# Attention of one decoder layer: dense causal scores per query block, or near key blocks plus key classes modulo 4

## The chip, the cores and the metric

The kernel runs on one core of one Trainium2 chip. The metric is the device time of one execution in microseconds; of the kernel before there are three runs, with a median of 1261.48 us (1261.13 to 1264.27). A core has one matrix engine (TensorE; PE in the profile, its weight loads as PEld), VectorE (DVE), ScalarE (ACT), GpSimd (POOL) and SyncE (SP), which issues the DMAs. Each engine works through its own queue in the order in which the program was written; semaphores hold an instruction until what it needs is there.

## The reference

One decoder layer on 1024 tokens of width 1024: RMS norm, one projection into two mixers (8 attention heads of width 64; 4 heads of a gated recurrence of width 128), an output projection, a residual, and a squared-ReLU MLP of width 4096. What the change touches is the attention. Query t sees key t - d with d >= 0 if one of three windows holds it, and the three branches are combined by their softmax denominators, which is one softmax over all keys with a bias that counts the windows:

```python
DILATED_PATTERNS = ((128, 1), (512, 4), (2048, 16))
d = np.arange(P)[:, None] + 896 - np.arange(T)[None, :]
ok = d >= 0
c = ((d <= 128) & ok).astype(np.float64) + ((d <= 512) & (d % 4 == 0) & ok) + ((d % 16 == 0) & ok)
tab[h] = np.where(c > 0, np.log(np.maximum(c, 1.0)) - slope * d, -1.0e30)
```

So for d over 128 only keys of the query's own class modulo 4 count; all others get the bias -1e30.

## The kernel before

The program is written out in full, and the order in which the Python code calls the engines is the order of every queue: a manual schedule. Numbers that need more than the matrix engine's short format are split into a high part and a low part; a product of two split numbers takes three matmuls (`three_pass`, lines 86 to 89), one of a split number and a short one takes two.

The stages are: the norm and the first projections; the four recurrent heads (`hgrn_core`), with projections of the next head filled in between; the attention, 8 heads in 4 pairs; the output projection, row by row of 128 tokens; the MLP.

**The attention loop before** (lines 1016 to 1049) makes 64 steps, one per head and block of 128 queries. In a step with block b:

- `score` multiplies the block's queries with all (b + 1) x 128 keys up to its own, in pieces of at most 512, each with the high and the low part of the keys (lines 703, 704; tile `ps`). VectorE adds the bias and takes the row maximum in one instruction (line 706).
- `expo` (line 717) is one ScalarE exponential over the whole row of keys, with its sum.
- `turn` (line 730, tile `pt`) transposes the weights block by block; ScalarE copies the high part out (`pth`, line 733), VectorE the low part (`ptl`, line 734).
- `weigh` (line 747, tile `pov`) multiplies the values with two query blocks at a time, 256 columns, once for the high and once for the low part.
- `finish` (lines 758 to 763) transposes the result back, adds the two halves and divides by the sum.

Between these steps `fill(ns)` takes work from a queue of generators until their stated costs use up a number of nanoseconds. The work is the projection of the next pair (`attn_proj`: 48 groups of three 512-column matmuls, tiles `pm_aq`, `pm_av`, `pm_ak`) and at the end the first half of the output projection for the first four rows (`early_out`, 32 groups, tile `pwe`). The allowance of a step falls with the block number (line 1045). `hooks` are calls tied to a step number: they load and split the weights of the output projection (`w_get`) and prepare its rows.

Biases (`bt`, 512 KB per head, line 683) and weights (`raw`, line 104) come by DMA on SyncE's queue. The two halves of q, kh and kl are also copied between the partitions of a pair's two heads by DMA (lines 589, 590, 619, 620).

Of the kernel before, what the change touches and what calls it, by code (L numbers as in the profile page):

```python
# [35 lines left out]
def hymba_layer(ctx, tc, x, w_in, w_out, w_ff1, w_ff2, g_pre, lb_logits, g_mix, g_post,  # L36
# [114 lines left out]
    for i in range(4 * HH, 4 * HH + 3 * (AH // 2)):  # L151
        stream.append((w_in[i], None))
    WO0 = len(stream)
    WO_TAG = (None, None, ("S", "S"), ("S", "BT"), ("S", "S"), ("S", "T"), ("T", "T"), ("T", "T"))
# [262 lines left out]
    def hgrn_core(h, scale, after=None):  # L417
# [143 lines left out]
        fill(1500 * scale)  # L561
# [8 lines left out]
    first_done = [False] * (AH // 2)  # L570
    A0 = 4 * HH

    put_off = []

    def keys_read(pr, pm, hf):
# [3 lines left out]
        return full  # L579

    def keys_off(pr, stacks, full, hf):

        sl = slice(hf * 512, hf * 512 + 512)
# [8 lines left out]
    def keys_late():  # L592
        while put_off:
            pr, stacks, src, hf, read = put_off.pop()
            keys_off(pr, stacks, src if read else keys_read(pr, src, hf), hf)

    def keys_early_read():
        pr, stacks, src, hf, _ = put_off.pop()
        put_off.append((pr, stacks, keys_read(pr, src, hf), hf, True))

    def attn_proj(pr):
# [5 lines left out]
        for hf in range(2):  # L607
            sl = slice(hf * 512, hf * 512 + 512)
            for n, cost in enumerate(proj_t(w, f"aq{pr}", hf, box)):
                if hf == 0 and n == 4:  # L610
                    w_get(A0 + 3 * pr)
                yield cost
# [8 lines left out]
            yield 650.0  # L621
        w = w_get(A0 + 3 * pr + 1, 0)
        vs = slab("V8", f"v{pr}", F32R, (P, NT, 2, 2, 64))
        late = None

        def v_turn(full, hf):
            pt = bank("mm", f"pvt{pr}{hf}")
            for j in range(4):
                TE.transpose(pt[:, j * P:(j + 1) * P], full[:, j * P:(j + 1) * P], ident)
            ptv = pt.rearrange("p (j h d) -> p j h d", j=4, h=2)  # L630
            dst = vs[:, hf * 4:hf * 4 + 4]
            S.activation(dst[:, :, :, 0, :], ptv, AF.Copy)
            V.tensor_tensor(out=dst[:, :, :, 1, :], in0=ptv, in1=f32(dst[:, :, :, 0, :]), op=ALU.subtract)
        for hf in range(2):
            sl = slice(hf * 512, hf * 512 + 512)
            n = 0
            for cost in proj_t(w, f"av{pr}", hf, box):
                n += 1
                if n == 4 and late is not None:
                    v_turn(*late)  # L640
                    cost += 450.0
                if n == 5 and hf == 0:
                    w_get(A0 + 3 * pr + 1)
# [4 lines left out]
            yield 650.0  # L648
        while pr > 0 and not first_done[pr - 1]:
            yield None  # L650
        w = w_get(A0 + 3 * pr + 2, 0)
        for i in range(2):
            stacks[i]["kh"] = slab("S", f"kh{pr}_{i}", F32R)
            stacks[i]["kl"] = slab("S", f"kl{pr}_{i}", F32R)
        for hf in range(2):
            sl = slice(hf * 512, hf * 512 + 512)
            n = 0
            for cost in proj_t(w, f"ak{pr}", hf, box):
                n += 1
                if n == 3 and hf == 0:  # L660
                    v_turn(*late)
                    cost += 450.0
                if n == 6 and hf == 0:
                    w_get(A0 + 3 * pr + 2)
                yield cost
            if hf == 0 and pr == AH // 2 - 1:
                early_rows()
            if hf == 0:
                keys_off(pr, stacks, keys_read(pr, box[0], hf), hf)
            else:  # L670
                put_off.append((pr, stacks, box[0], hf, False))
            pairs[pr] = (stacks, vs)
            yield 650.0

    anats = [None] * (AH // 2)
    bts = {}
    stats = {}
    pts = {}

    def load_bias(hd):  # L680
        if hd < AH and hd not in bts:
            bts[hd] = slab("BT", f"bt{hd}") if hd < AH - 1 else early["table"][:, 0]
            nc.sync.dma_start(out=bts[hd], in_=bias_tab[hd])

    def score(hd, b):
        stacks, _ = pairs[hd // 2]
        if b == 0:
            load_bias(hd)
            if hd + 1 < AH - 1:
                load_bias(hd + 1)  # L690
            stats[hd] = {n: tp.tile([P, NT, 2] if n == "mx" else [P, NT], F32, tag=n, name=f"{n}{hd}", bufs=2)
                         for n in ("mx", "nm", "dn", "rd")}
        q, kh, kl = (stacks[hd % 2][n] for n in ("q", "kh", "kl"))
        nk = (b + 1) * P
        mx, nm = stats[hd]["mx"], stats[hd]["nm"]
        pe = slab("P", f"p{hd}_{b}")
        pieces = []
        qs = q[:, b * P:(b + 1) * P]
        for pc in range(1 if nk <= 512 else 2):
            k0 = pc * 512  # L700
            n = min(512, nk - k0)
            pS = bank("s", f"ps{hd}_{b}_{pc}")
            TE.matmul(pS[:, :n], qs, kh[:, k0:k0 + n], start=True, stop=False)
            TE.matmul(pS[:, :n], qs, kl[:, k0:k0 + n], start=False, stop=True)  # L704
            o = 896 - b * P + k0
            V.tensor_tensor_reduce(out=pe[:, k0:k0 + n], in0=pS[:, :n], in1=bts[hd][:, o:o + n], scale=1.0,  # L706
                                   scalar=-3.0e38, op0=ALU.add, op1=ALU.max, accum_out=mx[:, b, pc:pc + 1])
            pieces.append((k0, n))
        if len(pieces) == 1:
            V.tensor_scalar(nm[:, b:b + 1], mx[:, b, 0:1], -1.0, None, op0=ALU.mult)  # L710
        else:
            V.tensor_scalar(nm[:, b:b + 1], mx[:, b, 0:1], mx[:, b, 1:2], -1.0, op0=ALU.max, op1=ALU.mult)
        return pe, nk

    def expo(hd, b, pe, nk):
        nm, dn = stats[hd]["nm"], stats[hd]["dn"]
        S.activation(pe[:, :nk], pe[:, :nk], AF.Exp, bias=nm[:, b:b + 1], accum_out=dn[:, b:b + 1])  # L717
        return pe

    def turn(hd, b, pe):  # L720
        g, u = divmod(b, 2)
        if u == 0:
            ns = (2 * g + 5) // 4
            pts[hd, g] = [[slab("T", f"pt{q}{hd}_{g}_{s}", F32R, (P, 4, 256)) for q in "hl"] for s in range(ns)]
        for s in range((b + 4) // 4):
            nj = min(4, b + 1 - 4 * s)
            pt = bank("t", f"pt{hd}_{b}_{s}")
            for j in range(nj):
                jj = s * 4 + j
                TE.transpose(pt[:, j * P:(j + 1) * P], pe[:, jj * P:(jj + 1) * P], ident)  # L730
            src = pt[:, :nj * P].rearrange("p (j c) -> p j c", j=nj)
            hi, lo = (q[:, :nj, u * P:(u + 1) * P] for q in pts[hd, g][s])
            S.activation(hi, src, AF.Copy)  # L733
            V.tensor_tensor(out=lo, in0=src, in1=f32(hi), op=ALU.subtract)  # L734
        dn, rd = stats[hd]["dn"], stats[hd]["rd"]
        V.reciprocal(rd[:, b:b + 1], dn[:, b:b + 1])

    def weigh(hd, g):
        _, vs = pairs[hd // 2]
        pt = pts.pop((hd, g))  # L740
        po = bank("pv", f"pov{hd}_{g}")
        nj = 2 * g + 2
        for j in range(nj):
            c0 = P if j == nj - 1 else 0
            vst = vs[:, j, hd % 2].rearrange("p a d -> p (a d)")
            for q in range(2):
                TE.matmul(po[:, c0:256], vst, pt[j // 4][q][:, j % 4, c0:],  # L747
                          start=j == 0 and q == 0, stop=j == nj - 1 and q == 1)
        ot = sp.tile([P, 256], F32, tag="ot", name=f"ot{hd}_{g}", bufs=1)
        S.activation(ot, po[:, :256], AF.Copy)  # L750
        return po, ot

    def finish(hd, g, po, ot):
        pr = hd // 2
        if anats[pr] is None:
            anats[pr] = slab("T", f"anat{pr}", F32, (P, NT, 2, 64))
        for u in range(2):
            TE.transpose(po[:, 256 + u * P:256 + (u + 1) * P], ot[:, u * P:(u + 1) * P], ident)
        pair = po[:, 256:].rearrange("p (u a d) -> p u a d", u=2, a=2)
        b = slice(2 * g, 2 * g + 2)  # L760
        dst = anats[pr][:, b, hd % 2]
        V.tensor_reduce(dst, pair.rearrange("p u a d -> p u d a"), axis=AX.X, op=ALU.add)  # L762
        G.tensor_tensor(out=dst, in0=dst, in1=stats[hd]["rd"][:, b].unsqueeze(2).to_broadcast([P, 2, 64]),  # L763
                        op=ALU.mult)
        if hd % 2 and g == NT // 2 - 1 and pr < AH // 2 - 1:
# [1130 lines left out]
```

## Time and profile before

| | |
|---|---|
| three runs | 1261.13, 1261.48, 1264.27 us |
| the profiled execution, span | 1258.5 us |
| PE busy | 1235.4 us (98%) |
| DVE, ACT, POOL busy | 884.6 (70%), 531.9 (42%), 300.6 us (24%) |
| DMA, share of 16 engines | 36.0% on the queue that SyncE issues |
| the attention loop in the profile | 307 us to 557 us |

The profiled execution's span is 3.0 us under the median of the runs. "Busy" of PE counts each matmul with the time that its result needs to come out, and these overlap: matmuls that follow each other can each last longer than the distance between their starts. The distance of two starts is what a matmul costs in a sequence. Time in which PE waits less than that overlap shows as no idle time at all.

### The profile page before, as it was taken

The page shows a single profiled execution, that of the slowest core. Times are in us where ns is not written, and L with a number is a line of the kernel's source. Part 1 is how long each engine was busy: PE and PEld are TensorE (multiplying, and loading weights), DVE is VectorE, ACT ScalarE, POOL GpSimd, SP SyncE. Part 2 cuts the span into 40 slices and gives each one's busy share as a digit, 9 for nine tenths or more (in the row PEclk, how much of TensorE's full clock was granted, in tenths as well). Part 3 has the DMA queues.
Part 4 walks back from the last instruction along what each step waited for, and adds up shares of the span by engine and source line. Part 5 has one row for each costly group of instructions (what it writes and reads, how often), then busy time and mean ns, then how long its engine had stood idle before and what let it go on. Part 6 is the DMA issues. An engine that isn't in the chain of part 4 may idle for free. (4 is left out here: it accounts for less than half of the span.)

```text
span 1258.5 us, 17252 instructions
## 1 busy us (share of the span) xinstructions
PE 1235.4 (98%) x6512; PEld 1056.1 (84%) x6512; DVE 884.6 (70%) x1535; ACT 531.9 (42%) x970; POOL 300.6 (24%) x303
## 2 busy tenths in 40 slices
PE   8999999999999999999999999999999999999997
PEld 8898989888888887878878788888878888888886
DVE  5686868675666667668759756666685777698966
ACT  7523232222555556666565322222237434444412
POOL 0000000012222223146250487656621000000012
PEclk9999999999999999999999999999999999999999
DMA  5201111122322224245242545434468454434423
GB/s 210 68 18 51 34 52 34 35 84 64 89 71 81 69 83 132 81 133 184 101 150 81 207 164 184 155 135 172 149 249 324 167 198 134 162 92 132 162 89 118
DMA packets 58578, 153.98 MB, mean 122 GB/s; under 512 B 4992, under 2 KB 12928, under 8 KB 58240
## 3 DMA queue, kind: packets, MB, share of 16 engines
q1 hardware_dynamic: 58496, 152.89, 36.0%
q8 instruction: 51, 0.84, 0.3%
q14 instruction: 31, 0.25, 0.1%
HBM read 106.73 MB, written 39.85 MB: 116 GB/s over the span
## 5 line engine op out<-in xcount | busy, mean ns | idle before, releaser
L87 PE MATMUL f<-bh,ah 128*128 128x512 f32 x392 | 152.5, 389 | 0.0
L88 PE MATMUL f<-bl,ah 128*128 128x512 f32 x392 | 152.5, 389 | 0.0
L89 PE MATMUL f<-bh,al 128*128 128x512 f32 x392 | 152.5, 389 | 0.0
L84 DVE TENSOR_TENSOR al<-ar,ah 128x1024 fp32r<-128x1024 f32 x49 | 60.7, 1238 | 48.1 <-ACT ah L83 19.4
L89 PEld LDWEIGHTS f<-bh,al 128*128 128x128 f32 x392 | 73.6, 188 | 15.4
L87 PEld LDWEIGHTS f<-bh,ah 128*128 128x128 f32 x392 | 73.6, 188 | 15.3
L88 PEld LDWEIGHTS f<-bl,ah 128*128 128x128 f32 x392 | 73.6, 188 | 15.1
L83 ACT ACTIVATE ah<-ar 128x1024 fp32r<-128x1024 f32 x49 | 52.1, 1063 | 50.2 <-PE f L89 25.3
L1814 POOL TENSOR_SCALAR fp<-fss 128x1 f32<-128x1 f32 x8 | 3.7, 462 | 269.4 <-ACT fd L1810 269.4
L734 DVE TENSOR_TENSOR ptl<-pt,pth 128x512 fp32r<-128x512 f32 (+2 forms) x96 | 50.4, 553 | 23.4 <-ACT pth L733 23.3
L733 ACT ACTIVATE pth<-pt 128x512 fp32r<-128x512 f32 (+2 forms) x96 | 43.3, 487 | 40.0 <-PE pt L730 38.5
L706 DVE CUSTOM_DVE_ANT_0 p<-ps,bt 128x512 f32<-128x512 f32 (+2 forms) x84 | 44.4, 554 | 18.3 <-PE ps L704 18.1
L1313 POOL TENSOR_TENSOR e<-x,e 128x512 f32<-128x512 f32 x14 | 20.6, 1475 | 136.0 <-DVE x L1264 136.0
L79 POOL TENSOR_SCALAR ms<-hss 128x8 f32<-128x8 f32 x4 | 0.8, 198 | 209.2 <-DVE hss L554 209.2
L717 ACT ACTIVATE p<-p,nm 128x128 f32<-128x128 f32 (+3 forms) x64 | 49.4, 772 | 2.5 <-DVE nm L710 2.1
L83 ACT ACTIVATE bh<-br 128x1024 fp32r<-128x1024 f32 x28 | 29.8, 1064 | 43.1 <-PE f L89 37.7
L763 POOL TENSOR_TENSOR anat<-anat,rd 128x128 f32<-128x128 f32 x32 | 14.7, 461 | 131.8 <-DVE anat L762 130.9
L730 PE MATMUL pt<-ident,p 128*128 128x128 f32 x288 | 42.7, 275 | 2.7 <-DVE ptl L734 1.6
L747 PE MATMUL pov<-pth,v 128*128 128x256 f32 (+1 forms) x160 | 40.3, 287 | 1.3 <-ACT pth L733 1.3
L1667 DVE TENSOR_TENSOR acc<-f,acc 128x512 f32<-128x512 f32 x52 | 33.8, 686 | 8.2 <-PE f L89 8.2
L730 PEld LDWEIGHTS pt<-ident,p 128*128 128x128 f32 x288 | 33.3, 141 | 7.2 <-DVE ptl L734 3.5
L83 ACT ACTIVATE bh<-tt 128x1024 fp32r<-128x1024 f32 x21 | 22.3, 1061 | 38.2 <-PE f L89 22.9
(1622 smaller groups left out, 3902.3 us busy)
## 6 DMA issues: line engine op xcount, KB each, us to landing
ar<-actd SPq DMA_DIRECT2D x49, 512.0 KB, 3.7
raw<-in_w_in_dram SPq DMA_DIRECT2D x28, 512.0 KB, 3.6
w1r<-in_w_ff_dram SPq DMA_DIRECT2D x14, 1024.0 KB, 6.2
br<-in_w_ff_dram SPq DMA_DIRECT2D x14, 1024.0 KB, 7.9
actd<-e SPq DMA_DIRECT2D x17, 768.0 KB, 4.1
actd<-e SPq DMA_DIRECT2D x11, 1024.0 KB, 4.0
xr<-in_x_dram SPq DMA_DIRECT2D x8, 512.0 KB, 8.6
raw<-in_w_out_dram SPq DMA_DIRECT2D x8, 512.0 KB, 3.6
```

The costliest lines, as they stand in the source:

```text
L83: S.activation(hi, src, AF.Copy)
L84: eng.tensor_tensor(out=lo, in0=src, in1=f32(hi), op=ALU.subtract)
L87: TE.matmul(dst, lhs[0], rhs[0], start=start, stop=False)
L88: TE.matmul(dst, lhs[0], rhs[1], start=False, stop=False)
L89: TE.matmul(dst, lhs[1], rhs[0], start=False, stop=stop)
L706: V.tensor_tensor_reduce(out=pe[:, k0:k0 + n], in0=pS[:, :n], in1=bts[hd][:, o:o + n], scale=1.0, scalar=-3.0e38, op0=ALU.add, op1=ALU.max ...
L717: S.activation(pe[:, :nk], pe[:, :nk], AF.Exp, bias=nm[:, b:b + 1], accum_out=dn[:, b:b + 1])
L730: TE.transpose(pt[:, j * P:(j + 1) * P], pe[:, jj * P:(jj + 1) * P], ident)
L733: S.activation(hi, src, AF.Copy)
L734: V.tensor_tensor(out=lo, in0=src, in1=f32(hi), op=ALU.subtract)
L747: TE.matmul(po[:, c0:256], vst, pt[j // 4][q][:, j % 4, c0:], start=j == 0 and q == 0, stop=j == nj - 1 and q == 1)
L1667: V.tensor_tensor(out=acc_at(p, i), in0=pm, in1=acc_at(p, i), op=ALU.add)
```

## The change

The queries of the first half (blocks 0 to 3) keep their dense scores. A query block of the second half is scored in two parts. The **near** part takes whole key blocks: keys 384 to 639 for block 4, 512 to 767 for block 5, 512 to 895 for block 6, 512 to 1023 for block 7. The **class** part takes the 512 queries of the second half and the 512 keys of the first half, both sorted by their number modulo 4, and multiplies only like with like: four products of 128 queries with 128 keys.

A query now has two row maxima in two layouts: by block (query 128 b + p on partition p) and by class (query 4 m + c on partition m). `exchange` writes both to DRAM and reads each back in the other layout, `shift` takes the larger of the two, and so both parts use one maximum. `sums` sends the sum of the class part the same way, and `recip` adds the two before the division.

Weighted values are now formed by key block: one transposed key block of all the query blocks that see it (up to 512 columns) against that block's values. In the second half the columns are kept in class order by a permuted unit matrix, `spare["turn"]`, and the values of the first half are also turned in class order (`vc`, four more transposes per pair). Keys are projected before values.

The loop is written new. There is one unit of work per head and half: `near_slot` for the first half's unit, `far_slot` for the second's, four steps each, so 64 steps again. Between pieces stands `yield 1`, at which one group of the queue is issued (`pump`), three per step; from step 46 on the rate is 0.67 of that. The one `fill` behind the last recurrent head is gone, and six groups are issued before the loop instead. The bias table is cut to what is read and comes in five DMAs per head. Hook numbers, and which buffers the output projection's first weights take, are moved.

```diff
@@ attn_proj: keys before values, values of the first half also by class
+        vc = slab("T", f"vc{pr}", F32R, (P, 4, 2, 2, 64))
...
+                TE.transpose(pt[:, j * P:(j + 1) * P], by_class(full)[:, j] if kind else full[:, j * P:(j + 1) * P], ident)
@@ tables, near key blocks, classes
+    FAR = ((384, 256), (512, 256), (512, 384), (512, 512))
+    def load_table(hd):
+        t = tabs[hd] = slab("BT", f"tab{hd}") if hd < AH - 1 else early["table"][:, 0]
...
+        nc.sync.dma_start(out=t[:, :512], in_=bias_tab[hd][:, 512:])
+        G.memset(t[:32, 896:], -1.0e30)
+        for b in range(4):
+            nc.sync.dma_start(out=t[32 * b:32 * b + 32, 512:1024 if b else 896], in_=src[:, 384 - P * b:896 - P * b if b else 768])
+    def score(hd, *blocks):
...
+        for b in blocks:
+            k0, n = keys_of(b)
+            two(pS[:, o:o + n], q[:, b * P:(b + 1) * P], kh[:, k0:k0 + n], kl[:, k0:k0 + n])
...
+    def score_classes(hd):
...
+        for c in range(4):
+            two(pS[:, c], by_class(q[:, 512:])[:, c], by_class(kh[:, :512])[:, c], by_class(kl[:, :512])[:, c])
...
+            row_max(probs["c"][:, c], pS[:, c], tab, unit(2 * hd + 1)["mx"][:, 4 + c:5 + c])
+    def exchange(u):
+        r = unit(u)
+        xd = dp.tile([2, 512], F32, name=f"xd{u}")
+        nc.sync.dma_start(out=xd[0].rearrange("(b p) -> p b", b=4), in_=r["mx"][:, :4])
+        nc.sync.dma_start(out=xd[1].rearrange("(m c) -> m c", c=4), in_=r["mx"][:, 4:])
+        nc.sync.dma_start(out=r["nm"][:, 4:], in_=xd[0].rearrange("(m c) -> m c", c=4))
+        nc.sync.dma_start(out=r["nm"][:, :4], in_=xd[1].rearrange("(b p) -> p b", b=4))
+    def shift(u):
...
+        if u % 2:
+            V.tensor_tensor(out=r["mx"], in0=r["mx"], in1=r["nm"], op=ALU.max)
+        V.tensor_scalar(r["nm"][:, w], r["mx"][:, w], -1.0, None, op0=ALU.mult)
@@ weighted values by key block: (key block, first query block, place in the turned tile, query blocks)
+    SUMS = (([(0, 0, 0, 4)], [(1, 1, 0, 3)], [(2, 2, 0, 2), (3, 3, 2, 1)]),
+            ([(4, 0, 0, 4)], [(5, 1, 0, 3), (3, 0, 3, 1)], [(6, 2, 0, 2), (7, 3, 2, 1)], None))
@@ the loop
-        fill(3240.0 - 340.0 * b if s < n_steps - 20 else 1000.0 if s < n_steps - 16 else 1175.0 if s != n_steps - 3 else 1.0,
-             b == 7 and s < n_steps - 20)
+    EARLY_GROUPS, LATE_FROM = 6, 46
+    LATE_RATE = (0.67,) * (n_steps - LATE_FROM)
+    def near_slot(hd):
...
+        score(hd, 7)
+        score_classes(hd)
+        exchange(u + 1)
...
+            load_table(nxt)
+        yield 1
+        turn(u, 1)
+        yield 1
+        weigh(u, 0)
+        yield 1
+        yield 0
+        turn(u, 2)
+        yield 1
+        weigh(u, 1)
+        yield 1
+        yield 1
+        yield 0
+        weigh(u, 2)
+        gather(u)
+        recip(u)
+        shift(u + 1)
+        expo(u + 1, 0, 1, 2, 3)
+        yield 1
+        yield 1
+        yield 1
+        yield 0
+    def far_slot(hd):
...
+            scores_d(nxt, 0)
+        yield 1
+        finish(u - 1)
+        yield 1
+        turn(u, 0)
...
```

How the rows of PE change: of the kernel before, one step of the loop, with the scores of block 5 against 768 keys in two pieces, four turned pieces of block 3 and a run of fillers (`pm_ak` is the projection, `pt` the turned weights):

```order
L703 MATMUL ps_5_0_4888<-kh_1_4072,q_1_3618 128x512
L704 MATMUL ps_5_0_4888<-kl_1_4073,q_1_3618 128x512
L703 MATMUL ps_5_1_4892<-kh_1_4072,q_1_3618 128x256
L704 MATMUL ps_5_1_4892<-kl_1_4073,q_1_3618 128x256
L730 MATMUL pt_3_0_4897<-ident,p_3_4788 128x128 x4
L758 MATMUL pov_0_4843<-ident,ot_0_4848 128x128 x2
L87 MATMUL pm_ak_4882<-hTh_92,wh_4595 128x512
L88 MATMUL pm_ak_4882<-hTl_93,wh_4595 128x512
L89 MATMUL pm_ak_4882<-hTh_92,wl_4596 128x512
```

And of the changed kernel the second step of a near slot: block 7 against 512 keys, the class scores, then groups of fillers between the pieces (`pm_av` is the projection, `pov` the weighted values):

```order
L704 MATMUL ps_7_3369<-kh_1_2667,q_1_2549 128x512
L705 MATMUL ps_7_3369<-kl_1_2668,q_1_2549 128x512
L704 MATMUL psc_3373<-kh_1_2667,q_1_2549 128x128
L705 MATMUL psc_3373<-kl_1_2668,q_1_2549 128x128
...
L87 MATMUL pm_av_3326<-hTh_90,wh_3187 128x512
L88 MATMUL pm_av_3326<-hTl_91,wh_3187 128x512
L89 MATMUL pm_av_3326<-hTh_90,wl_3188 128x512
L797 MATMUL pt_1_3408<-ident,prob_2544 128x128
L797 MATMUL pt_1_3408<-ident,prob_2948 128x128 x2
...
L818 MATMUL pov_3417<-pt_0_3349,v_2787 128x512 x2
```

Fewer and in part wider matmuls stand there, and eight narrow ones (the `psc` pair comes four times) that the kernel before does not have.

On SyncE's queue the kernel before has one bias load per head between the copies of kl and the next weights:

```order
L590 DMA kl_1_3364<-kl_1_3364 64x512
L683 DMA bt_3605<-in_bias_tab_dram 128x1024
L589 DMA kh_0_3361<-kh_0_3361 64x512
L590 DMA kh_1_3363<-kh_1_3363 64x512
L589 DMA kl_0_3362<-kl_0_3362 64x512
```

The changed kernel has there, once per head, the exchange of the maxima (`umx` to DRAM `xd`, `xd` to `unm`), five loads of the table, and before the next head the sums (`udn`, `nd`, `udd`):

```order
L744 DMA xd_3386<-umx_3335 128x4x1
L745 DMA xd_3386<-umx_3335 128x4
L746 DMA unm_3336<-xd_3386 128x4
L747 DMA unm_3336<-xd_3386 128x4x1
L677 DMA tab_3391<-in_bias_tab_dram 128x512
L680 DMA tab_3391<-in_bias_tab_dram 32x384
L680 DMA tab_3391<-in_bias_tab_dram 32x512 x3
L104 DMA raw_3405<-in_w_in_dram 128x1024
L766 DMA nd_3538<-udn_3337 128x4
L767 DMA udd_3338<-nd_3538 128x4x1
```

The reads from `xd` stand behind the writes, so they hold the queue until these have landed; the table and the next weights stand behind the reads.

On VectorE the larger maximum is taken in queue order, between other heads' and other pieces' work:

```order
L801 TENSOR_TENSOR pt_2_3423<-pt_2_3424,pt_2_3423 128x384
L663 TENSOR_TENSOR vf_3433<-pm_av_3326,rrow 128x512
L650 TENSOR_TENSOR v_3324<-pvt_3444,v_3324 128x8x64
L775 RECIPROCAL urd_3181<-udn_3179 128x4
L753 TENSOR_TENSOR umx_3335<-umx_3335,unm_3336 128x8
L754 TENSOR_SCALAR unm_3336<-umx_3335 128x8
L650 TENSOR_TENSOR vc_3325<-pvt_3469,vc_3325 128x8x64
L708 ISA prob_2948,umx_3484<-ps_0_3479,tab_3391 128x128
```

Line 753 waits for the exchange, and the rest of VectorE's queue stands behind it; in the kernel before, the maximum of a block is used on the spot and no DMA lies between.

More of the change, by code (lines that the diff above doesn't have):

```diff
@@ L647, in attn_proj @@
             late = (full, hf)
[L648 to L665, printed above, removed]
@@ L715, in expo @@
[L715 to L736, printed above, removed]
@@ L759, in finish @@
[L759 to L765, printed above, removed]
+        po = r["po"]
+        for j in range(4):
+            TE.transpose(po[:, j * P:(j + 1) * P], spare["ot"][:, j * P:(j + 1) * P], ident)
```

402 lines of the change are left out of this document (259 added, 143 removed).

## The prediction

> **What bounds the kernel now.** I read the page first, then the sums of the attention stage, then who makes PE wait there.
>
> ```profile
> span 1258.5 us, 17252 instructions
> ...
> PE 1235.4 (98%) x6512; PEld 1056.1 (84%) x6512; DVE 884.6 (70%) x1535; ACT 531.9 (42%) x970; POOL 300.6 (24%) x303
> ```
>
> ```profile
> core 0: us, PE busy (x) PEld busy (x) DVE busy (x) ACT busy (x) POOL busy (x), PEclk, DMA share, GB/s
> 307.00:557.00 250.00, 242.72 (x1449) 211.57 (x1448) 164.99 (x502) 148.66 (x330) 62.84 (x78) 0.99 0.28 82
> ```
>
> ```profile
> PE pmt L848 <- POOL erows L808: 2.9, 1, 2.9
> PE pt L730 <- DVE ptl L734: 1.6, 4, 1.0
> PE pov L747 <- ACT pth L733: 1.3, 1, 1.3
> PE pt L730 <- DVE mt L84: 1.0, 1, 1.0
> PE pov L747 <- DVE ptl L734: 0.3, 1, 0.3
> ```
>
> In the 250 us of the attention PE is busy for 242.7, VectorE for 165.0, ScalarE for 148.7, and all of PE's waits are 7.1 us (2.9 + 1.6 + 1.3 + 1.0 + 0.3). So matmuls taken out here shorten the stage, as long as the other engines and the DMAs still deliver in time.
>
> **What a matmul costs** is the distance to the next start, read in one stretch of the timeline (start, duration, instruction):
>
> ```profile
> 400.12 1.03 PE L730 MATMUL pt<-ident,p 128*128 128x128 f32 x8
> ...
> 401.68 0.40 PE L89 MATMUL pm_av<-hTh,wl 128*128 128x512 f32 x1
> 401.91 0.34 PE L703 MATMUL ps<-kh,q 128*128 128x384 f32 x1
> 402.09 0.34 PE L704 MATMUL ps<-kl,q 128*128 128x384 f32 x1
> ...
> 404.19 0.28 PE L747 MATMUL pov<-pth,v 128*128 128x256 f32 x1
> 404.31 0.28 PE L747 MATMUL pov<-ptl,v 128*128 128x256 f32 x1
> 404.43 0.22 PE L747 MATMUL pov<-pth,v 128*128 128x128 f32 x1
> 404.49 0.28 PE L747 MATMUL pov<-ptl,v 128*128 128x128 f32 x1
> 404.60 0.45 PE L87 MATMUL pm_av<-hTh,wh 128*128 128x512 f32 x1
> 404.88 0.39 PE L88 MATMUL pm_av<-hTl,wh 128*128 128x512 f32 x1
> ```
>
> 512 columns take 0.23 us (401.68 to 401.91), 384 take 0.18, 256 take 0.12. A transpose takes (1.03 - 0.28) / 7 = 0.108, its own duration being about that of a narrow matmul. Of the narrow pair the first takes 0.06, the second 0.11, and the matmul behind it is 0.05 late (0.28 where 0.23 is usual): 0.11 each. So narrow matmuls are dear: 128 columns cost almost what 256 do.
>
> **The matmuls, part by part.** The counts follow from the code. Per head, before, the scores are 12 of 512 columns and 4 each of 384, 256 and 128; after, they are 4 of 512, 4 of 384, 6 of 256 and 10 of 128 (eight of them classes): -8 x 0.23 + 2 x 0.12 + 6 x 0.11 = -0.94 us. The weighted values are 32 of 256 and 8 of 128 before (4.72 us); after, 4 of 512, 4 of 384, 4 of 256 and 14 of 128 (0.92 + 0.72 + 0.48 + 1.54 = 3.66 us): -1.06. Turned weights are 36 pieces before and 25 after: -11 x 0.108 = -1.19. Over 8 heads -7.5, -8.5 and -9.5. The values turned by class add 16 transposes, +1.7. Turning the results back stays at 8 transposes per head. The fillers stay what they are: 144 projection groups and 32 output groups move between steps, and the `fill` behind the last recurrent head only hands its groups to the loop. Sum: **-23.8 us**.
>
> **The other engines** keep their cover. Their rows:
>
> ```profile
> L734 DVE TENSOR_TENSOR ptl<-pt,pth 128x512 fp32r<-128x512 f32 x48 | 32.4, 689 | 16.3 <-ACT pth L733 16.3
> ...
> L706 DVE CUSTOM_DVE_ANT_0 p<-ps,bt 128x512 f32<-128x512 f32 x42 | 28.4, 688 | 14.2 <-PE ps L704 14.2
> L733 ACT ACTIVATE pth<-pt 128x512 fp32r<-128x512 f32 x48 | 27.7, 595 | 23.1 <-PE pt L730 21.5 <-POOL anat L763 1.2
> ...
> L717 ACT ACTIVATION_READ_ACCUMULATOR p<-p,nm 128x1 f32 x64 | 12.1, 189 | 0.0
> ...
> L706 DVE DVE_READ_ACCUMULATOR2_ANT mx<- 128x1 f32 x96 | 8.0, 83 | 0.0
> ...
> L717 ACT ACTIVATE p<-p,nm 128x512 f32<-128x512 f32 x8 | 5.7, 714 | 0.4 <-DVE nm L710 0.4
> ...
> L710 DVE TENSOR_SCALAR nm<-mx 128x1 f32<-128x1 f32 x32 | 4.9, 154 | 1.1
> L717 ACT ACTIVATE p<-p,nm 128x384 f32<-128x384 f32 x8 | 4.9, 611 | 0.1
> ...
> L717 ACT ACTIVATE p<-p,nm 128x256 f32<-128x256 f32 x8 | 4.1, 510 | 0.1
> ...
> L706 DVE CUSTOM_DVE_ANT_0 p<-ps,bt 128x128 f32<-128x128 f32 x14 | 4.0, 286 | 0.2
> ```
>
> VectorE loses about as many score columns as PE and keeps 12 row maxima per head; ScalarE's exponentials go from 8 to 12 per head, of narrower rows, and four more reads of the sum (4 x 0.19 us) are paid by fewer copied pieces. Neither comes near the share that PE has, so their work costs nothing; what may cost is when it is done.
>
> **The added wait: the exchange of the maxima.** Four small DMAs through DRAM, two hops in a row. Nothing that small is in this trace; the nearest landings:
>
> ```profile
> kl<-kl SPq DMA_DIRECT2D x16, 128.0 KB, 2.4
> ...
> ident<-in_ident_dram SPq DMA_DIRECT2D x1, 64.0 KB, 1.9
> gpre<-in_g_pre_dram SPq DMA_DIRECT2D x1, 4.0 KB, 3.4
> ```
>
> A hop lies between 1.9 us (`ident`) and 3.4 (`gpre`, few bytes in 128 pieces, behind other loads). I take 2.4, the row of this stage that is also a partition-wise shuffle; the exchange's pieces of 4 bytes speak for more.
>
> Now the chain of one head, counted from the moment PE starts block 7 in the near slot. Score 7 costs 0.46 us on PE, and its row maximum can begin 0.16 later (a 512-column result takes 0.39 for a distance of 0.23) and ends at 0.62 + 0.69 + 0.08 = 1.39; four class maxima of 0.29 + 0.08 end at 2.9. Two hops of 2.4: 7.7. Two small operations of 0.15 on VectorE: 8.0. Four exponentials (0.51 + 0.51 + 0.61 + 0.71 and 4 x 0.19): 11.1. Then PE may turn the first pieces of the second half.
>
> PE itself gets there after the rest of that step (0.46 + 8 x 0.11 + 3 groups of 0.69 + 3 transposes + 2 x 0.23 = 4.2 us), the next (0.32 + 0.36 + 2.07 = 2.75), the next (0.24 + 0.22 + 2.07 = 2.53) and the head of the far slot (0.46 + 0.43 + 1.38 = 2.27): 11.7 us. So the wait ends 0.6 us ahead, for six heads. Heads 6 and 7 have only 0.67 of the groups: 11 x 0.33 x 0.69 = 2.5 us less, and PE is there at 9.2, 1.9 us too early. What is queued behind the wait: on VectorE the low parts and the next head's row maxima, on SyncE the table, weights and sums; PE waits for all of them only a step later.
>
> Price: 2 x 1.9 = 3.8 us in the last two heads, and half a microsecond each in the other six for copies and weights ahead of the exchange in the queue: 7 us. Against it, 3.2 of the 7.1 us of waits go (the ones on `pth` and `ptl`): every turned piece now has two groups or more ahead of its use. The waits on `erows` and `mt` (3.9) belong to the output rows, which are prepared as before. Net **+4**. At 1.9 us a hop the six heads are covered and the last two lose 0.9 each: -1. At 3.4 a hop the chain ends at 13.1: 1.4 x 6 + 3.9 x 2 = 16.2, net +13.
>
> **Strided operands.** The class scores read every fourth column, as weights and as moving data, 64 matmuls, and so do 16 transposes. The nearest row is the last recurrent head's first level, which moves every second column:
>
> ```profile
> L502 PE MATMUL pl<-qt,kt x112: 217/275/275, 259.4 to 293.2; 128*128 128x64 f32 x112
> ```
>
> Minimum, median and maximum show no level that is slower, so I take zero; if a strided load took twice its time, 80 x 0.11 = 9 us.
>
> [...]
>
> **Sum.** 1258.5 - 23.8 + 4 = 1238.7 us for the profiled execution. The median of the three runs (1261.48) lies 3.0 above the profiled span, so 1241.7.
>
> **Rivals.**
>
> *The exchange is slow* (slower than before). From a hop of h the six heads lose 2h - 5.4 each and the last two 2h - 2.9. With 3.2 us of old waits gone, the gain is eaten when 16h - 38.2 = 27, at h = 4.1 us. At 4.8, twice the row taken, it is 38.6 - 3.2 - 23.8 = +11.6: 1273. For it: 512 pieces of 4 bytes on one side of each hop, and no such transfer in the trace. Against it: 64 KB land in 1.9 us, so the bytes are nothing.
>
> *The exchange at 3.4 us a hop*: 1258.5 - 23.8 + 13 + 3.0 = 1251.
>
> *Everything is hidden*: at 1.9 us a hop, 1258.5 - 23.8 - 1 + 3.0 = 1237. For it: all but the last two heads have cover already at 2.4.
>
> *Strided reads cost double*: 1241.7 + 9 = 1251. For it only that no row has such a step.
>
> *Fewer matmuls do not help*, because each shorter run is followed by a hidden wait for ScalarE and VectorE (copy and subtraction, 0.6 + 0.69 us for each turned piece): 1258 to 1265. Against it: two groups of 0.69 us stand between a turned piece and its use.
>
> **How the numbers follow.** Forecast 0.40; hidden 0.18; 3.4 us a hop 0.17; strided 0.10; fewer matmuls in vain 0.06; slow exchange 0.09. Four of these are faster (0.85). About 0.3% (3.8 us) is what a measurement can tell from no change, so "same" is 1257.7 to 1265.3: 0.06, and slower 0.09. The range 1228 to 1258 takes in all the faster cases, with some room below for waits that vanish unseen (those shorter than a matmul's result takes show as no idle time), and leaves out the last two. The forecast's own is 1237 to 1247.
>
> **What would show it.** The attention stage from the first score to the last result should shrink from 250 to about 230 us, PE's busy time by about 24, and the rest of the span should stay. Right: 312 transposes and 64 class scores with starts 0.11 us apart; PE's waits on `pt` of the second half's units near zero up to head 5 and about 2 us in heads 6 and 7; VectorE's wait at line 753 under a microsecond. Wrong: class scores 0.2 us apart (strided); landings of `xd` and `unm` over 4 us, with PE's fillers exhausted behind VectorE's queue; a lower granted clock from longer pauses; or a stage that stays at 250 us though PE's busy time in it falls.

## The result, and the profile after

The change makes the kernel slower: 1301.70 us (median of four runs, 1299.34 to 1302.67) beside 1261.61 before, a ratio of 1.031 (95% interval 1.030 to 1.033). The forecast was 1241.7, its range 1228 to 1258.

The page of the profiled execution, and the attention and what follows it as a table of windows (length, then busy time and count of each engine, the granted clock, the share of the DMA engines, GB/s):

```profile
span 1298.2 us, 16844 instructions
...
PE 1244.2 (96%) x6328; PEld 1052.0 (81%) x6328; DVE 854.8 (66%) x1404; ACT 522.1 (40%) x982; POOL 295.0 (23%) x295
```

```profile
307.00:592.00 285.00, 248.33 (x1263) 205.94 (x1262) 131.55 (x369) 137.56 (x340) 56.54 (x66) 0.93 0.28 72
592.00:1298.20 706.20, 695.22 (x3108) 573.90 (x3106) 506.03 (x552) 271.70 (x400) 217.98 (x207) 0.99 0.45 161
```

The attention takes 285 us where it took 250. PE executes 186 matmuls fewer in it (1449 before, 1263 now) and yet is "busy" for longer, because the granted clock is 0.93: at half speed the projection's matmuls of 512 columns start 0.43 us apart (476.61 and 477.04 us in this trace), at full speed 0.23. Behind the stage 706.2 us remain, where there were 701.5.

The waits in the stage, sorted by who waits (total, times, longest):

```profile
ACT prob L760 <- DVE unm L754: 50.6, 9, 8.3
DVE umx L753 <- DMA unm<-xd: 47.3, 7, 8.5
...
PE pt L797 <- ACT prob L760: 31.3, 25, 6.1
```

```profile
SPq L746 <- DMA xd<-umx: 55.7, 8, 8.8
```

Read from the bottom: SyncE stands 7 us per head at line 746 until the written maxima have landed, VectorE waits for what is read back, ScalarE for VectorE, PE for ScalarE. The landings in the stage, from issue, as medians:

```profile
xd<-umx SPq DMA_DIRECT2D x16, 2.0 KB, 8.4
unm<-xd SPq DMA_DIRECT2D x16, 2.0 KB, 3.2
nd<-udn SPq DMA_DIRECT2D x8, 2.0 KB, 2.1
udd<-nd SPq DMA_DIRECT2D x8, 2.0 KB, 2.3
```

`xd<-umx` is the slow one: the row maxima by block go out in 512 pieces of 4 bytes (line 744), those by class in 128 pieces of 16 (line 745) right behind them. `nd<-udn` is as many bytes in 16-byte pieces, alone, and lands in 2.1. The rows of the two writes apart, from issue to landing:

```profile
L744 SPq DMA_DIRECT2D xd<-umx x8: 370/378/539, 322.3 to 558.5; - x8
DMA to landing us min/median/max: 8.1/8.9/11.4
```

```profile
L745 SPq DMA_DIRECT2D xd<-umx x8: 332/335/425, 323.0 to 561.1; - x8
DMA to landing us min/median/max: 5.8/7.6/10.1
```

One head of the trace, by engine (start, duration; in brackets the idle time before it and who ended it), and the same stretch in windows:

```profile
458.70 0.53 SPq L744 DMA_DIRECT2D xd<-umx  x1
460.97 0.33 SPq L745 DMA_DIRECT2D xd<-umx  x1
470.11 0.33 SPq L746 DMA_DIRECT2D unm<-xd  x1
...
471.14 0.49 SPq L677 DMA_DIRECT2D tab<-in_bias_tab_dram  x1
```

```profile
473.05 0.17 DVE L753 TENSOR_TENSOR umx<-umx,unm 128x8 f32<-128x8 f32 x1 [8.45 <-DMA unm<-xd]
```

```profile
469.62 0.40 PE L89 MATMUL pm_ak<-hTh,wl 128*128 128x512 f32 x1
474.11 1.57 PE L797 MATMUL pt<-prob,prob 128*128 128x128 f32 x3 [4.09 <-ACT prob L760]
```

```profile
470.00:474.00 4.00, 0.02 (x1) 0.00 (x0) 0.34 (x2) 0.54 (x3) 0.00 (x0) 1.00 0.39 95
474.00:480.80 6.80, 6.32 (x18) 4.66 (x19) 4.14 (x10) 4.17 (x11) 0.82 (x2) 0.50 0.47 132
```

From the write at 458.7 to the larger maximum at 473.1 pass 14.4 us. PE has nothing left for 4.5 us (start to start), and then works for 6.8 us at clock 0.50. In the whole stage 41 us run at half speed (the table's 0.93 says as much: 0.07 x 285 x 2 = 40), where 3.4 did before. Half of that, some 20 us, is lost on top of the waiting. This is an estimate and a little high, since 3.4 of the 41 us lie inside PE's pauses.

The stage's half-speed stretches last 3.4 or 6.8 us each. One of 3.4 us (511.6 to 515.0) followed a pause of 2.3 us (PE's starts at 506.90 and 509.21) and three of 0.5 to 0.7. The longest pause alone does not decide it. In experiment 1 below, 6.8 us at half speed (from 484.6 us) follow three pauses of 0.6, 1.1 and 1.4 us within 4 us, and a later pause of 2.35 us (531.78 to 534.14) brings none. What does decide it is not shown.

Lastly the class scores, in one head:

```profile
354.80 0.41 PE L705 MATMUL psc<-kl,q 128*128 128x128 f32 x1
355.03 0.41 PE L704 MATMUL psc<-kh,q 128*128 128x128 f32 x1
```

```profile
L704 PEld LDWEIGHTS ps<-kh,q x64: 186/188/338, 307.7 to 556.9; 128*128 128x128 f32 x64
...
L704 PEld LDWEIGHTS psc<-kh,q x32: 308/329/332, 319.6 to 558.7; 128*128 128x128 f32 x32
```

They start 0.23 us apart, as far as matmuls of 512 columns, and their weight loads take 329 ns (median) where loads of neighbouring columns take 188.

### The profile page after: what moved, and what is told of

Same layout as the page of the kernel before. It is cut to its first block, busy times and chain, and to the rows that moved or that the text cites. A ratio compares the mean times of both kernels' runs of the same rounds, so it can differ in the third digit from the quotient of the medians.

```text
span 1298.2 us, 16844 instructions
## 1 busy us (share of the span) xinstructions
PE 1244.2 (96%) x6328; PEld 1052.0 (81%) x6328; DVE 854.8 (66%) x1404; ACT 522.1 (40%) x982; POOL 295.0 (23%) x295
## 5 line engine op out<-in xcount | busy, mean ns | idle before, releaser
L760 ACT ACTIVATE prob<-prob,unm 128x128 f32<-128x128 f32 (+2 forms) x96 | 48.4, 506 | 50.6 <-DVE unm L754 50.6
L801 DVE TENSOR_TENSOR pt<-pt,pt 128x512 fp32r<-128x512 f32 (+1 forms) x56 | 35.1, 631 | 34.3 <-ACT pt L800 34.3
L797 PE MATMUL pt<-prob,prob 128*128 128x128 f32 x88 | 24.3, 360 | 31.8 <-ACT prob L760 31.3
L800 ACT ACTIVATE pt<-pt 128x512 fp32r<-128x512 f32 (+1 forms) x56 | 30.6, 550 | 59.3 <-PE pt L797 57.1
L797 PEld LDWEIGHTS pt<-prob,prob 128*128 128x128 f32 x88 | 14.5, 172 | 43.4 <-ACT prob L760 41.0
L840 POOL TENSOR_TENSOR anat<-anat,urd 128x256 f32<-128x256 f32 x16 | 9.8, 614 | 138.5 <-DVE anat L839 138.5
L83 ACT ACTIVATE bh<-tt 128x1024 fp32r<-128x1024 f32 x21 | 22.3, 1060 | 37.9 <-PE f L89 22.5
L84 DVE TENSOR_TENSOR wl<-raw,wh 128x1024 fp32r<-128x1024 f32 x23 | 28.1, 1222 | 12.7 <-ACT wh L83 12.4
L84 DVE TENSOR_TENSOR bl<-br,bh 128x1024 fp32r<-128x1024 f32 x28 | 34.2, 1221 | 2.9 <-PE f L88 2.5
```

The costliest lines, as they stand in the source:

```text
L84: eng.tensor_tensor(out=lo, in0=src, in1=f32(hi), op=ALU.subtract)
L760: S.activation(pe, pe, AF.Exp, bias=r["nm"][:, j:j + 1], accum_out=r["dn"][:, j:j + 1])
L797: TE.transpose(pt[:, j * P:(j + 1) * P], src, spare["turn"] if hf and kb != "c" else ident)
L800: S.activation(hi, ptv, AF.Copy)
L801: V.tensor_tensor(out=lo, in0=ptv, in1=f32(hi), op=ALU.subtract)
L840: G.tensor_tensor(out=dst, in0=dst, in1=r["rd"].unsqueeze(2).to_broadcast([P, 4, 64]), op=ALU.mult)
```

## The experiments

**Theory**: the loss is the exchange of the maxima, and in it the write in 4-byte pieces; a smaller part is the strided class scores. **Rivals**: the strided operands carry most of it; or the matmuls taken out were worth nothing. All edits are against the changed kernel unless another is named.

**1. No exchange.** The second half's softmax subtracts no maximum.

```diff
 def exchange(u):
+    return
     ...
 def shift(u):
     ...
-    if u % 2:
-        V.tensor_tensor(out=r["mx"], in0=r["mx"], in1=r["nm"], op=ALU.max)
-    V.tensor_scalar(r["nm"][:, w], r["mx"][:, w], -1.0, None, op0=ALU.mult)
+    V.tensor_scalar(r["nm"][:, w], r["mx"][:, w], 0.0 if u % 2 else -1.0, None, op0=ALU.mult)
```

> Leaves out the exchange of the maxima: the second half's exponentials are taken without subtracting a maximum, so no DMA and no wait lies between scores and exponentials. Theory 1 (the exchange is what costs): PE's 31 us of waits for the exponentials go, and with them most of the half-speed clock of the attention stage (granted clock 0.93 over 285 us, 20 us): 1245 to 1258 us. Theory 2 (the class scores' strided reads cost most): 1290 us or more.

1248.65 us, ratio to before 0.990 (0.988 to 0.992). The exchange costs 1301.7 - 1248.7 = 53.0 us. The stage takes 233 us, at a clock of 0.99:

```profile
308.00:541.00 233.00, 227.73 (x1254) 195.76 (x1253) 129.55 (x360) 137.22 (x339) 56.02 (x66) 0.99 0.32 88
```

**2. Class scores on neighbouring columns**, exchange as it was. The scores are then others than the layer needs; only the time counts here, and so it is in experiments 3 and 6.

```diff
-    two(pS[:, c], by_class(q[:, 512:])[:, c], by_class(kh[:, :512])[:, c], by_class(kl[:, :512])[:, c])
+    f, g = slice(c * P, c * P + P), slice(512 + c * P, 640 + c * P)
+    two(pS[:, c], q[:, g], kh[:, f], kl[:, f])
```

> The class scores read blocks of 128 neighbouring columns in place of every fourth, the same number and size of matmuls on other data; the exchange stays. Theory 1: 64 matmuls fall from 0.23 to 0.11 us, 7.7 us, and the exchange starts 0.9 us earlier in each head: 1286 to 1294 us, PE still waits over 20 us for exponentials. Theory 2: most of the loss goes: 1265 us or less.

1308.55 us, ratio to before 1.037 (1.035 to 1.038): slower than the changed kernel, though the class scores became cheaper (their weight loads 191 ns on average). A miss for every theory.

```profile
PE pt L798 <- ACT prob L761: 42.5, 19, 7.3
```

```profile
308.00:602.00 294.00, 245.72 (x1253) 201.79 (x1252) 130.68 (x368) 136.65 (x339) 55.44 (x66) 0.88 0.27 70
```

PE waits 42.5 us in place of 31.3, and the clock falls from 0.93 to 0.88. The trace shows two sides of it. PE reaches the wait earlier, since the class scores got shorter, and the two writes landed later (medians 9.6 and 8.9 us, where the changed kernel has 8.9 and 7.6):

```profile
L745 SPq DMA_DIRECT2D xd<-umx x8: 371/377/539, 322.7 to 569.0; - x8
DMA to landing us min/median/max: 8.7/9.6/12.6
```

From the start of the first class score to the larger maximum pass 15.2 us (mean of the eight heads), 14.4 in the changed kernel. The pauses grow, and 68 us of the stage run at half speed in place of 41. Why the writes landed later stays open, and no run isolates what each part costs.

**3. Both edits.**

```diff
 def exchange(u):
+    return
     ...
 def score_classes(hd):
     ...
+    two(pS[:, c], q[:, g], kh[:, f], kl[:, f])
```

> Both edits: no exchange, and class scores on neighbouring columns. If these two are all that was wrong, what is left is the prediction's term for the matmuls, -23.8 us, and some waits: 1235 to 1245 us. A third cause would leave it above 1250.

1240.27 us, ratio 0.983 (0.981 to 0.984). Without a wait in front of it, the stride costs 1248.65 - 1240.27 = 8.4 us. What is left of the change is worth 1261.8 - 1240.3 = 21.5 us: the matmuls that were taken out do shorten the stage.

**4. The write in 16-byte pieces.** The maxima by block are written in the order in which they lie in SBUF, and four reads sort them.

```diff
-    nc.sync.dma_start(out=xd[0].rearrange("(b p) -> p b", b=4), in_=r["mx"][:, :4])
+    nc.sync.dma_start(out=xd[0].rearrange("(p b) -> p b", b=4), in_=r["mx"][:, :4])
     ...
-    nc.sync.dma_start(out=r["nm"][:, 4:], in_=xd[0].rearrange("(m c) -> m c", c=4))
+    for b in range(4):
+        nc.sync.dma_start(out=r["nm"][32 * b:32 * b + 32, 4:],
+                          in_=xd[0].rearrange("(i c b) -> b i c", i=32, c=4)[b])
```

> The exchange stays whole, but the block maxima are written to DRAM as 16 bytes per partition and put in the other order by the reads (four small reads in place of one). Theory 1a (the 512 scattered 4-byte writes are slow, 8 to 11 us): the writes land in 1.5 to 3 us and the time comes within 12 us of the kernel without exchange: 1250 to 1268 us. Theory 1b (any way through DRAM is too slow, or the queue behind it): 1285 us or more.

1261.35 us, ratio 0.999 (0.998 to 1.000).

```profile
unm<-xd SPq DMA_DIRECT2D x32, 0.5 KB, 2.0
xd<-umx SPq DMA_DIRECT2D x16, 2.0 KB, 2.1
unm<-xd SPq DMA_DIRECT2D x8, 2.0 KB, 2.3
```

```profile
PE pt L799 <- ACT prob L762: 5.6, 11, 2.4
```

The same bytes land in 2.1 us, and 40.4 of the exchange's 53.0 us are gone; 12.7 stay. (The profiled execution is one of the quicker ones, 1258.97 us.) The piece size of one write is the largest single cause. By the access patterns the edit does not remove the 512 pieces of 4 bytes, it moves them from the write to the four reads (4 x 128), and in 4-byte pieces the reads land in 2.0 to 2.3. So the write shows the cost of small pieces (8.9 us at line 744 of the changed kernel, 2.1 here, medians), and the reads do not.

**5. The exchange sent, but waited for by nobody.** The reads land in a tile that nothing uses, and `shift` is that of experiment 1.

```diff
+    got = tp.tile([P, 8], F32, tag="got", name=f"got{u}", bufs=2)
     ...
-    nc.sync.dma_start(out=r["nm"][:, 4:], in_=xd[0].rearrange("(m c) -> m c", c=4))
-    nc.sync.dma_start(out=r["nm"][:, :4], in_=xd[1].rearrange("(b p) -> p b", b=4))
+    nc.sync.dma_start(out=got[:, 4:], in_=xd[0].rearrange("(m c) -> m c", c=4))
+    nc.sync.dma_start(out=got[:, :4], in_=xd[1].rearrange("(b p) -> p b", b=4))
```

> The four transfers of the exchange are issued as in the changed kernel, but land in a tile that nothing reads; the second half's exponentials are taken without subtracting a maximum (this part of the computation is left out), so nothing waits for the transfers except the next head's reuse of the tile. Theory (waiting for the maxima costs, not the transfers on SyncE's queue): close to the kernel without an exchange (1248.7 us), so 1249 to 1253, stage near 233 us, half-speed time near 7 us. Rival (the four transfers hold up others on SyncE's queue, or the memory behind it): 1275 or more, with waits for sums, tables or weights in the stage that the kernel without an exchange did not have.

1283.95 us, ratio 1.018 (1.017 to 1.020). The theory falls here: a wait for the maxima is not needed for a loss of 35 us.

```profile
DVE prob L708 <- DMA tab<-in_bias_tab_dram: 41.2, 6, 11.1
...
PE ps L704 <- DVE umx L708: 16.7, 8, 6.1
```

```profile
422.22 0.34 SPq L746 DMA_DIRECT2D xd<-umx  x1
429.47 0.33 SPq L747 DMA_DIRECT2D got<-xd  x1
429.90 2.75 SPq L748 DMA_DIRECT2D got<-xd  x1
432.70 0.50 SPq L677 DMA_DIRECT2D tab<-in_bias_tab_dram  x1
```

SyncE issues in order. Its read waits for the write (422.2 to 429.5), and the next head's bias table, needed for the row maxima, stands behind that read. VectorE waits 41.2 us for the table, and PE 16.7 us at its scores for VectorE's row maxima. (The 2.75 us at line 748 are an exception; the median of the eight heads is 0.39.)

**6. Which operand's stride costs.** No exchange; only the stationary operand q from neighbouring columns.

```diff
-    two(pS[:, c], by_class(q[:, 512:])[:, c], by_class(kh[:, :512])[:, c], by_class(kl[:, :512])[:, c])
+    g = slice(512 + c * P, 640 + c * P)
+    two(pS[:, c], q[:, g], by_class(kh[:, :512])[:, c], by_class(kl[:, :512])[:, c])
```

> No exchange (second half's exponentials without subtracting a maximum), and of the class scores only the stationary operand q is taken from neighbouring columns; the moving operands keep every fourth column, so the output differs from the reference. With both operands strided the time was 1248.7, with neither 1240.3. Theory (the weight loads cost, since their strided form took 329 ns against 188 and the strided matmul rows overlap them): 1239 to 1242, the starts of the class scores near 0.12 us apart. Rival (the moving operands' stride costs): 1247 to 1250, starts near 0.23 us apart. Third: each takes its share, 1243 to 1246.

1241.51 us, ratio 0.984 (0.983 to 0.986): 1.2 above the run without any stride (1240.3), and the two intervals overlap. The starts are 0.12 apart again, with moving operands that still take every fourth column:

```profile
319.85 0.30 PE L704 MATMUL psc<-kh,q 128*128 128x128 f32 x1
319.96 0.30 PE L705 MATMUL psc<-kl,q 128*128 128x128 f32 x1
```

**7. The near part's maximum alone**, sent ahead of the class scores; only the class exponentials, which come later, use what was sent.

```diff
-    for c in range(4):
-        row_max(probs["c"][:, c], pS[:, c], tab, unit(2 * hd + 1)["mx"][:, 4 + c:5 + c])
+    V.tensor_tensor(out=probs["c"], in0=pS, in1=tab.unsqueeze(1).to_broadcast([P, 4, P]), op=ALU.add)
     ...
+    nc.sync.dma_start(out=xd.rearrange("(p b) -> p b", b=4), in_=r["nm"][:, :4])
+    for b in range(4):
+        nc.sync.dma_start(out=r["ne"][32 * b:32 * b + 32], in_=xd.rearrange("(i c b) -> b i c", i=32, c=4)[b])
     score(hd, 7)
-    score_classes(hd)
+    shift(u + 1)
     exchange(u + 1)
+    score_classes(hd)
     ...
```

> The shared maximum is the near part's alone: it is negated right after score 7 and sent ahead of the class scores by one write of 16-byte pieces and four reads; the near exponentials wait for no transfer, the class exponentials come later and alone read what was sent; the four class row maxima become one addition of 512 columns on VectorE. All of the computation is done. Theory (the wait for the landing and the half-speed clock behind it are the loss, and a landing of about 5 us is covered by the near exponentials and their turns): near the kernel without an exchange, 1244 to 1251 us, no wait of PE for the exponentials over 1 us per head, half-speed time near 7 us. Rival (any landing in the chain of a head is felt, since SyncE issues five transfers of 0.4 to 0.6 us): 1255 to 1265, like the kernel with the 16-byte writes (1261).

1247.91 us, ratio 0.989 (0.987 to 0.991), as without an exchange (1248.65). The edit is more than an earlier exchange: one addition also stands in place of four row maxima on VectorE. All the waits of PE in the stage are these; none is on the exchange:

```profile
PE pov L814 <- DVE pt L797: 2.1, 4, 1.0
PE pmt L920 <- DVE pt L797: 2.0, 1, 2.0
PE pov L814 <- ACT pt L796: 0.9, 1, 0.9
```

**8 and 9. A sorted copy of q** on top of 7, made by GpSimd right ahead of score 7 (8, shown), and two pieces earlier, behind `turn(u, 0)` (9).

```diff
+def sort_q(hd):
+    t = qcs[hd] = half(f"qc{hd}", F32R).rearrange("p (c n) -> p c n", c=4)
+    G.tensor_copy(t, f32(by_class(q[:, 512:])))
     ...
-    two(pS[:, c], by_class(q[:, 512:])[:, c], by_class(kh[:, :512])[:, c], by_class(kl[:, :512])[:, c])
+    two(pS[:, c], qcs[hd][:, c], by_class(kh[:, :512])[:, c], by_class(kl[:, :512])[:, c])
     ...
+    sort_q(hd)
     score(hd, 7)
```

> As the kernel with the near part's maximum alone, and with the second half's q of each head copied once, by GpSimd, into class order ahead of score 7, so that the class scores take their stationary operand from neighbouring columns; the moving operands keep their stride. All of the computation is done. Theory (the strided weight loads cost 64 times 0.11 us in the stage and a copy on GpSimd is hidden): 1247.9 less 7, so 1239 to 1243. Rival (the copy or the buffer that it takes from the projections holds PE up): 1246 to 1252, with waits of PE for the copy or of the projections' pieces for their buffer in the stage's list of waits.

> As the kernel with the sorted copy of q, with the copy two steps earlier in the head (ahead of the finish of the unit before). All of the computation is done. Theory of the hidden copy: 1239 to 1243, the same as with the later copy within 2 us. If PE waits for the copy in the later place, this one is faster by that wait; if the projections wait for the buffer, this one is slower, 1245 or more.

Late copy: 1265.08 us, ratio 1.002 (1.000 to 1.003). Early copy: 1248.00, 0.989 (0.988 to 0.990). The late copy is waited for in every head, the early one in the first only (the rows of the one and of the other):

```profile
PE psc L704 <- POOL qc L736: 13.7, 8, 3.1
```

```profile
PE psc L704 <- POOL qc L736: 3.1, 1, 3.1
```

So the rival of experiment 8 held in kind, as PE waits for the copy, but its range (1246 to 1252) was too low by far: the late copy cost 17 us (31 us of its stage run at half speed, 7 without the copy). The early one is 17 us faster, where the two rows of waits differ by 10.6, and gains nothing over experiment 7; the theory of the hidden copy falls in both places.

**10. The bias table ahead of the exchange** on SyncE, against experiment 5.

```diff
     score_classes(hd)
-    exchange(u + 1)
     ...
         load_table(nxt)
+    exchange(u + 1)
```

> As the kernel whose exchange is sent but waited for by nobody (1284.0; the second half's exponentials subtract no maximum, that part is left out), with one edit: the load of the next head's bias table stands ahead of the exchange's four transfers on SyncE instead of behind them. Theory (those 1284 came from the table's load, held in SyncE's order behind the wait for the scattered write: 41.2 us of waits for the table): 1249 to 1256, waits for the table under 5 us. Rival (the scattered writes load the memory or the DMA engines whatever stands behind them): 1270 or more, with landings of other transfers longer than in the kernel without an exchange.

1261.66 us, ratio 1.000 (0.999 to 1.001): 22.3 of the 35.3 us that experiment 5 lost against no exchange at all come back, the waits for the table are gone, and 13.0 us stay, more than the theory gave. The trace shows other followers of the same wait. In one head, on SyncE, ScalarE and PE:

```profile
524.76 0.33 SPq L746 DMA_DIRECT2D xd<-umx  x1
532.04 0.33 SPq L747 DMA_DIRECT2D got<-xd  x1
532.47 2.18 SPq L748 DMA_DIRECT2D got<-xd  x1
534.74 1.41 SPq L876 DMA_DIRECT2D row<-mixd  x3
```

```profile
537.82 0.52 ACT L894 ACTIVATE dm<-row 128x384 f32<-128x384 f32 x1 [5.86 <-DMA row<-mixd]
```

```profile
539.26 1.73 PE L817 MATMUL pov<-pt,v 128*128 128x384 f32 x4 [4.62 <-ACT pt L799]
```

Rows of the output projection, issued behind the exchange, hold ScalarE, and with it the copy of turned weights that PE needs. This is one head; in another PE waits 2.9 us at its scores. That such waits make up the whole remainder was not tried.

**11 and 12. The early copy on ScalarE**, for all heads, and (the last edit) for all but the first.

```diff
-    G.tensor_copy(t, f32(by_class(q[:, 512:])))
+    S.activation(t, f32(by_class(q[:, 512:])), AF.Copy)
     ...
-    sort_q(hd)
+    if hd:
+        sort_q(hd)
```

> As the kernel with the early sorted copy of q (1248.0, no better than the 1247.9 without it), with the copy on ScalarE instead of GpSimd. All of the computation is done. Theory (the copy gains 7 us in the class scores and lost them again on GpSimd: 3.5 us of waiting in the first head, where the copy stood behind a subtraction of 2.6 us, the half-speed clock behind that pause, and 0.9 us on VectorE while GpSimd copied): 1240 to 1244, no wait of PE for the copy over 0.5 us. Rival (the copy's gain in the class scores is taken back wherever the copy runs, because it holds a buffer of the projections): 1246 to 1250.

> As the kernel with q copied on ScalarE (1247.1), but the first head takes its stationary operand with the stride, without a copy; the other seven heads use the copy. All of the computation is done. The traces show the first head's copy waiting for the projections' buffer (PE stood 3.5 us from start to start, and the clock was at half for 6.8 us around it). Theory (that one pause ate the gain): 1247.1 less 3.5 less half of 6.8 and more 0.9 for the stride in one head, so 1240 to 1243. Rival (the gain is lost elsewhere): 1245 to 1249.

1247.07 us, ratio 0.989 (0.987 to 0.990), and 1243.33, ratio 0.985 (0.984 to 0.987). Moving the copy to ScalarE changed next to nothing, so the theory of experiment 11 falls. In the first head the copy waits, on ScalarE too, until GpSimd has finished `ql`, and PE still waits 3.1 us:

```profile
322.24 1.11 ACT L736 ACTIVATE qc<-q 128x512 fp32r<-128x512 f32 x1 [1.44 <-POOL ql L618]
```

Leaving the first head out gained 3.7 us; the time is 0.3 above the range expected. Against experiment 7 the copy in seven heads is worth 4.6 us, where experiment 8 had hoped for 7 in all eight; the rest was not traced. Experiment 12 does all of the computation and is the fastest such kernel here, 18.3 us ahead of the kernel before.

## Why the prediction was wrong

**The step that failed is the added wait.** The price of a hop was bounded between 1.9 and 3.4 us by landings of transfers with contiguous pieces, and taken as 2.4; the write measured 8.4 (median of both, 8.9 for the 4-byte one) and the read 3.2. The working had itself said that pieces of 4 bytes "speak for more" and then let no bound go past 3.4. The rival "the exchange is slow" named the cause and had the break-even, 4.1 us a hop; measured were (8.4 + 3.2) / 2 = 5.8. Its own formula gives 16 x 5.8 - 38.2 - 3.2 = 51.4 us, where taking the exchange out gave 53.0. That agreement is partly luck: PE's waits on the exponentials are 31.3 us, not the 54.6 of the formula's losses. Counted from the start of block 7, PE arrives after 12.7 to 13.6 us in the first six heads, where 11.7 was forecast, and the wait ends after 14.4 to 17.2 us, where the formula at 5.8 us a hop has 17.9. The slowed clock adds to the waits. From the first score to the last result the stage is 50.6 us longer than in experiment 1 (285.0 and 234.4): 26.7 more in pauses of PE over half a microsecond (31.2 and 4.5), and half of 34 us more at half speed (41.0 and 6.8), 17.1. That leaves 6.8 us not assigned, or 8.5 if the 3.4 us at half speed inside pauses are not counted twice. The lower clock stood among the signs of being wrong, but with no term in the sum.

**The same step underrated the queue.** It listed the table, weights and sums behind the exchange on SyncE and priced them at nothing, as PE "waits for all of them only a step later". With a hop of 2.4 us that may hold. With a landing of 8 us the table alone is worth 22.3 us (experiments 5 and 10). In the changed kernel this hardly shows: VectorE's row maxima wait only 2.5 us for the table there (another 5.4 are put down to the table at line 753, which reads none). That the wait for the maxima ends later and covers the table is a reading, not shown by a run.

**Strided operands were taken as zero**, with 9 us as the other bound. Measured: 8.4 (experiments 1 and 3), for the reason named, slower loads of strided weights (329 ns in place of 188), in 64 matmuls that start 0.12 us further apart each (7.7 us). The row it rested on had a stride of two. The transposes of `vf` by class, every fourth column too, still start 0.11 to 0.12 apart, though their weight loads grow from 140 to some 200 ns. The stride cost in the stationary operand of the scores, 329 against 188 ns, and not visibly in the moving one (experiment 6: 1241.5 us, where 1240.3 without any stride).

**The matmul term was right in kind and nearly in size.** -23.8 us forecast; experiment 3, without exchange and stride, is 21.5 us faster than before (interval 20.1 to 23.7). Besides, 3.2 us of old waits were to go; PE's waits fell by 2.1 only, from 7.1 to 5.0 us in experiment 1. Experiment 3 also ran 6.8 us at half speed in the stage, before 3.4. So the rival "fewer matmuls in vain" is out, and the other engines kept their cover, as written: in experiment 7, too, PE waits no more than 5.0 us in the stage for them (2.1 + 2.0 + 0.9).

**Heads 6 and 7** do wait longest, as forecast (6.5 and 5.4 us from start to start). The six heads before them were taken as covered and paused for 1.1 to 4.5 us.

In one sum: experiment 3 at 1240.3, 8.4 for the stride, 53.0 for the exchange, together 1301.7. It holds in this order only: with the exchange in place, taking out the stride cost 6.9 us (experiment 2).

## What to carry to other kernels

Price a small write to DRAM by its pieces, not its bytes, and let the unknown's upper bound go as far as the reason against it points: here a write of 2 KB in 4-byte pieces took four times as long to land as the same bytes in 16-byte pieces (8.9 and 2.1 us; reads did not show it), and one rearrangement of the write was worth 40 us. A DMA that waited on SyncE's in-order queue delayed what was issued behind it (in experiment 5 VectorE waited 41.2 us for the table), so the wait that the profile shows may cover others of the same origin; ask what is late next once it is gone. Better than a faster exchange was to need less of it: one bound that is ready early (the near part's maximum) and used late left nothing of the 53 us.

## What the hardware showed that was not expected

- Writes to DRAM in 512 pieces of 4 bytes landed after 8.1 to 11.4 us; the 16-byte write issued behind took 5.8 to 10.1; in 16-byte pieces both took 2.1 (median). Reads in 4-byte pieces took 2.1 to 4.9 us in the changed kernel.
- A stationary operand that takes every fourth column loads in 329 ns in place of 188, and narrow matmuls then start 0.23 us apart in place of 0.12. The same stride in the moving operand cost nothing that could be seen (1241.5 us in experiment 6, 1240.3 without any stride).
- Making the class scores faster made the kernel slower (1308.6 and 1301.7 us): PE reached the wait earlier, the write landed later (9.6 and 8.9 us), and 68 us of the stage ran at half speed in place of 41. That these lost more than the scores gained is the reading that fits; no run takes them apart.
- Half speed does not go by the longest pause alone: it followed a pause of 2.3 us in the changed kernel, three pauses of at most 1.4 us in experiment 1, and not a pause of 2.35 us there.
